# Planning a fused decoder block's TensorE order in whole groups, with a price for changing the kind of matmul and a new table of instruction lengths

## The chip, the core and the metric

The kernel runs on one core of a Trainium2 chip. The core has five instruction streams that run side by side and wait for each other through semaphores: TensorE (PE in the profile, with its weight loads as PEld), VectorE (DVE), ScalarE (ACT), GpSimd (POOL) and SyncE (SP). SP and POOL issue the DMAs. Each stream executes its instructions strictly in the order in which the program lists them, so an instruction that waits holds up everything behind it on its engine. The metric is the time of one execution on the device in microseconds (us), the median of several runs.

## The reference

One layer of a hybrid decoder: a pooling mixer and a gated DeltaNet side by side, on 2048 tokens of width 1024, all in float32.

```python
n    = rms_norm(x, norm_w)
proj = n @ w_in                      # 24 column tiles of 128, and 8 gate columns
pu, pz, q, k, v, dz, b, a = split(proj)

# pooling branch: 4 groups of 128 channels, trailing windows 2, 4, 8, 16
mix    = trailing_mean(pu, w) - pu
y_pool = (mix @ pool_w[g]) * pool_scale * silu(pz)

# DeltaNet branch: 4 heads of 128
q, k, v = split(silu(causal_conv4(q, k, v)))
q, k    = l2_normalize(q), l2_normalize(k)
beta, g = sigmoid(b), -exp(a_log) * softplus(a + dt_bias)
o       = gated_delta_rule(q, k, v, g, beta)   # chunked, a triangular solve per chunk
y_dn    = rms(o) * norm_w * silu(dz)

h   = x + concat(y_pool, y_dn) @ w_out
out = rms_norm(h, final_norm_w)
```

The chunked rule computes, per chunk and head, a triangular matrix A = strict_lower(k_beta k^T * decay), its inverse T = (I + A)^-1, and then steps a 128 x 128 state from chunk to chunk: v_new = u - w S, o = q_dec S + qk v_new, S = S * decay + k_dec^T v_new.

## The kernel before, in words

The tokens are worked in two blocks of 1024, each in two halves of 512. For each of the 24 column tiles of the input projection and each half, a unit of 8 steps (one for each 128 rows of the weight, `project`, L623) accumulates a 128 x 512 result in one PSUM bank. Each operand is split into a high and a low float32r part, so a step is three matmuls: high weight by high input (L629), high weight by low input (L630), low weight by high input (L631). These wide float32r matmuls are the bulk of TensorE's work. The output projection at the end is made of the same triples (L1164 to L1166 for the first four token tiles, L1278 to L1280 for the others, which are worked in pairs with seven products in place of eight).

Between the units lies the DeltaNet work of each head. Its matmuls are of two other kinds. Full-width float32 matmuls and transposes have 128 output partitions: the transposes of k, q, v and of the output (L719, L930), the products k k^T and k q^T (L745, L783), and the steps of the state from chunk to chunk, `chain_k`, `chain_u` and `chain_s` (L884 to L910). A float32 matmul stands in the trace as two records, a transpose as one. Narrow matmuls write to 32 or 64 partitions: they build the triangular inverse from its 32 x 32 blocks in five groups per head, `level1_y` (L839, 32 records), `level1_x` (L851, 32 records), `level2_t` (L863, 8), `level2_y` (L870, 16) and `level2_x` (L877, 16). The inverse of the 32 x 32 blocks themselves is done on VectorE (L799, L805), between two trips through DRAM (`scatter`, L762 and L765, and `gather`, L817 and L822) that rearrange the blocks.

The order of the work is not the order of the source. Every piece is put on a list with `at(slot, fn, ...)`; such an entry is an event. A slot is one step of a unit. `trace_events` (L599) runs the events in order of slot, which emits all instructions in program order. Then `Planner.run` (L151) makes an order for every engine by a simulation of its own: `costs` (L119) says for each instruction how long it holds its engine and after how long its result can be used, `preds` holds what must be finished first, `begun` what must have been started first. PSUM writes into the same bank depend on each other in it, so that the next matmul of a unit counts as ready some 440 ns after the one before. `propose` (L241) picks the next instruction of an engine. For TensorE it looks at the ready instructions in program order, no further than REACH = 200 TensorE instructions beyond the first one not yet placed, and takes the first that is ready within 30 ns, each matmul by itself (L254). For the other engines it goes by latest start times that are worked back from TensorE's program order. `bind` (L316) then fixes the orders found, for all five engines. The plan decides orders alone; on the chip the semaphores decide the times.

Some buffers tie the heads together: k, q, z and the inverse have two buffers each, the values and outputs of a head (`v0`) one, so the next head's values are written only when the head before has been stored.

Of the kernel before, what the change touches and what calls it, by code (L numbers as in the profile page):

```python
# [8 lines left out]
F32R = mybir.dt.float32r  # L9
# [5 lines left out]
P = 128  # L15
# [5 lines left out]
HALF = 512  # L21
# [60 lines left out]
HOP, REACH, SLACK, AHEAD = 40, 200, 100, 30000  # L82
# [3 lines left out]
class Planner:  # L86
# [4 lines left out]
    def __init__(self, tc, traced):  # L91
        self.tc = tc
        self.behind, self.next_to = {}, {}
        self.psum = set()
        self.rings = {}
        self.traced = traced

# [21 lines left out]
    def costs(self, i, outs, ins):  # L119

        op, eng = i.opcode, i.engine.name
        n = 1
        for _, c in outs[0].bass_ap.ap[1:]:
            n *= c
        psum = any(a.bass_ap.tensor.name in self.psum for a in (*outs, *ins))
        if op == "DMACopy":
            total = n * outs[0].bass_ap.ap[0][1] * 4 / 1024
            run = min(a.bass_ap.ap[-1][1] if a.bass_ap.ap[-1][0] == 1 else 1 for a in (outs[0], ins[0])) * 4
            land = 2200 + total * (5.5 if run >= 512 else 8)
            if eng == "Pool":  # L130
                return (860, 2900 + total * 5.4) if len(ins) > 1 or str(i.cce_op) != "bypass" else (600, 2400 + total * 3)
            return 550, land
        if eng == "PE":
            full = ins[0].dtype == F32R
            if full:
                return max(n / 2.4 + 13, 60), max(n / 2.4 + 190, 300)
            if getattr(i, "is_transpose", False):
                return (110, 290) if n > 64 else (56, 235)
            return (max(1.71 * n, 62), max(1.7 * n + 180, 240)) if n < 512 else (860, 1040)
        if eng == "Activation":  # L140
            extra = 190 if len(outs) > 1 else 0
            base = (150 if psum or extra else 110) + 0.82 * n
            return base + extra, base + extra + 110
        if eng == "Pool":
            return (650, 700) if op == "TensorScalarAffineSelect" else (2.5 * n + 100, 2.5 * n + 150)
        if op == "StreamTranspose":
            return 1.2 * n + 30, 1.2 * n + 130
        base = (68 if op == "TensorTensor" else 122 if n > 8 else 78) + 1.05 * n
        return base, base + 95

    def run(self):  # L151
        L = [i for i in self.traced if i.engine.name in self.ENGINES and (len(i.outs) or len(i.ins))]
        L = [i for i in L if i.opcode not in ("TilePoolBoundary", "TileManualSchedule")]
        N = len(L)
# [3 lines left out]
        for k, i in enumerate(L):  # L158
# [10 lines left out]
            if i.opcode == "DMACopy" and str(i.cce_op) != "bypass":  # L169
                acc.append((outs[0], False))  # L170
            for a, w in acc:
# [6 lines left out]
                if name in every:  # L178
                    begun[k].add(every[name][0])
                    if name in self.psum and w:  # L180
                        begun[k].add(next((j for j in reversed(every[name]) if eng[j] == eng[k]), every[name][0]))
# [52 lines left out]
        pe = [k for k in range(N) if eng[k] == "PE"]  # L234
        head = 0
        done = [False] * N
        lag = 0.0
        left = N
        proposal = {}

        def propose(e):  # L241
            c = cand[e]
            if not c:
                return None
            f = free[e]
            if e == "PE":
                lim = pe[min(head + REACH, len(pe) - 1)]
                c.sort()
                best = None
                for k in c:  # L250
                    if k > lim:
                        break
                    r = max(f, ready[k])
                    if r <= f + 30:  # L254
                        return r, k
                    if best is None or r < best[0]:
                        best = (r, k)
                return best
# [4 lines left out]
            u = min(c, key=lambda k: late[k])  # L263
# [15 lines left out]

        dirty = set(self.ENGINES)  # L280
        while left:
# [4 lines left out]
            at, k = proposal[e]  # L286
            cand[e].remove(k)
            order[e].append(k)
            start[k] = at
            done[k] = True  # L290
            left -= 1
            s = step[k]
            if e == "Activation" and table[k] and table[k] != act:
                act = table[k]
                s += 1283
                at += 1283
            free[e] = start[k] + s
            fin = at + lat[k] + HOP
            if e == "SP":
                lanes.append(fin)  # L300
            if e == "PE":
                lag = max(0.0, at - late[k]) if k == pe[head] else lag
                while head < len(pe) and done[pe[head]]:
                    head += 1
            dirty.add(e)
            for nexts, when in ((succs[k], fin), (after[k], at)):
                for j in nexts:
                    ready[j] = max(ready[j], when)
                    waiting[j] -= 1
                    if not waiting[j]:  # L310
                        cand[eng[j]].append(j)
                        dirty.add(eng[j])
# [12 lines left out]
def hymba_kernel(  # L325
# [273 lines left out]
    def trace_events():  # L599
        for _, _, fn, args in sorted(events, key=lambda e: e[:2]):  # L600
            fn(*args)
# [807 lines left out]
```

## Time and profile before

| | |
|---|---|
| median of 3 runs | 1005.52 us (997.4 to 1012.31) |
| the profiled execution: device time | 1004.09 us |
| its span, first to last instruction | 1002.4 us |
| outside the span (the difference) | 1.7 us |
| mean granted TensorE clock | 0.983 |
| TensorE busy | 950.6 us of the span |
| VectorE, ScalarE, GpSimd busy | 647.8, 474.5, 149.6 us |

In the views, a row of the timeline gives the start and the length in us, the engine, the line, the operation, output and inputs, their shapes and how many instructions were merged into the row. A matmul's length there includes its way through the array, so two that follow each other overlap: the time that one costs is the distance from its start to the next one's start. A row of the groups by line gives the busy time of the group, the mean length of one in ns, and the idle time of the engine before them.

### The profile page before, as it was taken

What the parts mean: (1) busy time and instruction counts of PE and PEld (TensorE: products, weight loads), DVE (VectorE), ACT (ScalarE), POOL (GpSimd) and SP (SyncE); (2) the same over time, 40 slices, a digit from 0 to 9 for tenths busy, and PEclk for the clock granted to TensorE, in tenths of its full rate; (3) what the DMA queues carried; (4) which work ended last, traced back from release to release, by engine and by line L of the source; (5) the groups of instructions that cost most, each with busy time, mean ns of one, the idle gap of its engine ahead of it and who ended that gap; (6) DMA issues with size and microseconds to landing.
All of it is one profiled execution on the core that took longest, in us unless ns stands there. A gap on an engine that the chain in (4) does not pass through costs nothing.

```text
span 1002.4 us, 14877 instructions
## 1 busy us (share of the span) xinstructions
PE 950.6 (95%) x5180; PEld 754.5 (75%) x5180; DVE 647.8 (65%) x1954; ACT 474.5 (47%) x1212; POOL 149.6 (15%) x200
## 2 busy tenths in 40 slices
PE   4999989999999899999999999899999998899995
PEld 3768767878888678767888878778868776688884
DVE  6477765758658436765885875756824467758765
ACT  7337653455464435433855445445423334344442
POOL 3204300100101012202520010110001110011111
PEclk9999989999999899999999999999999999999998
DMA  7322543423533634533445343253347486457644
GB/s 253 77 56 56 113 106 65 80 68 90 111 79 66 167 96 121 121 79 65 109 91 116 69 100 69 64 111 79 68 99 203 138 231 209 147 137 163 176 102 127
DMA packets 80396, 112.17 MB, mean 112 GB/s; under 512 B 31680, under 2 KB 49344, under 8 KB 80320
## 3 DMA queue, kind: packets, MB, share of 16 engines
q0 software_dynamic: 18000, 59.25, 28.5%
q1 hardware_dynamic: 62320, 51.96, 17.2%
q8 instruction: 41, 0.67, 0.3%
q14 instruction: 35, 0.29, 0.1%
HBM read 92.31 MB, written 18.87 MB: 111 GB/s over the span
## 4 chain that ended last, share of the span: by engine, by line
PE 68%; DVE 9%; DMA 9%; issue 8%; ACT 2%; SPq 1%; POOL 1%; DVEq 0%; POOLq 0%; ACTq 0%
PE ps L629 14%; PE ps L631 14%; PE ps L630 14%; DMA wh<-in_w_in_dram 2%; PE tp L719 2%; PE ch L906 1%; PE ch L900 1%; PE ch L884 1%; PE ob L894 1%; PE kk L745 1%; PE p L877 1%; DVE acc L643 1%; PE ob L910 1%; PE psA L1278 1%; PE pm L692 1%
## 5 line engine op out<-in xcount | busy, mean ns | idle before, releaser
L629 PE MATMUL ps<-nh,wh 128*128 128x512 f32 x768 | 293.6, 422 | 13.9 <-ACT wh L617 10.8
L631 PE MATMUL ps<-nh,wl 128*128 128x512 f32 x768 | 294.8, 421 | 1.9 <-DMA wl<-in_w_in_dram 1.3
L630 PE MATMUL ps<-nl,wh 128*128 128x512 f32 x768 | 290.8, 418 | 0.0
L629 PEld LDWEIGHTS ps<-nh,wh 128*128 128x128 f32 x768 | 144.6, 192 | 43.6 <-ACT wh L617 11.2
L631 PEld LDWEIGHTS ps<-nh,wl 128*128 128x128 f32 x768 | 146.8, 192 | 31.2 <-DMA wl<-in_w_in_dram 2.2
L630 PEld LDWEIGHTS ps<-nl,wh 128*128 128x128 f32 x768 | 145.9, 192 | 27.7 <-issue 1.7
L643 DVE SCALAR_TENSOR_TENSOR acc<-u,cw,acc 128x512 f32<-128x512 f32 x144 | 110.7, 769 | 14.8 <-ACT acc L641 13.2
L612 POOL DMA_DIRECT2D wh<-in_w_in_dram x46 | 26.2, 569 | 347.7 <-PE ps L630 240.6
L621 POOL DMA_DIRECT2D wl<-in_w_in_dram x46 | 39.3, 855 | 250.9 <-ACT wl L620 173.7
L799 DVE TENSOR_TENSOR tmp<-Ai,X 128x60 f32<-128x60 f32 (+24 forms) x248 | 53.6, 216 | 13.1 <-DMA Ai<-blocks 7.8
L620 ACT ACTIVATE wl<-wh 128x1024 fp32r<-128x1024 f32 x46 | 48.6, 1057 | 19.1 <-DMA wh<-in_w_in_dram 15.9
L805 DVE TENSOR_TENSOR X<-X,tmp 128x60 f32<-128x60 f32 (+24 forms) x248 | 53.0, 214 | 5.7
L638 DVE TENSOR_TENSOR u<-ps,rb 128x512 f32<-128x512 f32 x48 | 33.0, 688 | 35.6 <-PE ps L631 33.2
L913 ACT ACTIVATE sqj<-v 128x128 f32<-128x128 f32 x64 | 19.7, 307 | 67.5 <-DVE v L911 57.3
L641 ACT ACTIVATE acc<-u,cw 128x512 f32<-128x512 f32 x48 | 34.9, 726 | 25.6 <-DVE u L638 22.5
L726 ACT ACTIVATE sqj<-tp 128x128 f32<-128x128 f32 x128 | 33.8, 277 | 13.7 <-PE tp L719 13.0
L896 ACT ACTIVATE o<-ob,ex 128x128 f32<-128x128 f32 x64 | 23.4, 366 | 32.1 <-PE ob L894 31.5
L1173 ACT ACTIVATE t<-dec 128x512 f32<-128x512 f32 x32 | 20.2, 631 | 38.8 <-DVE dec L1171 38.5
L886 DVE SCALAR_TENSOR_TENSOR rho<-ch,negc,v 128x128 f32<-128x128 f32 x64 | 22.3, 348 | 24.4 <-PE ch L884 22.6
L1286 POOL DMA_DIRECT2D dec<-in_x_dram x24 | 20.5, 853 | 117.5 <-ACT dec L1285 98.6
L902 ACT ACTIVATE nv<-ch,sm 128x128 f32<-128x128 f32 x64 | 23.4, 366 | 26.0 <-PE ch L900 24.3
L748 DVE SCALAR_TENSOR_TENSOR At<-kk,sm,dec 128x128 f32<-128x128 f32 x64 | 18.2, 345 | 26.3 <-PE kk L745 26.2
(289 smaller groups left out, 1801.9 us busy)
## 6 DMA issues: line engine op xcount, KB each, us to landing
wh<-in_w_in_dram POOLq DMA_DIRECT2D x46, 512.0 KB, 3.9
wl<-in_w_in_dram POOLq DMA_DIRECT2D x46, 512.0 KB, 5.5
y_dram<-yt SPq DMA_DIRECT2D x32, 256.0 KB, 3.3
out_dram<-dec SPq DMA_DIRECT2D x14, 512.0 KB, 3.3
dec<-in_x_dram POOLq DMA_DIRECT2D x24, 256.0 KB, 4.0
Ai<-blocks SPq DMA_DIRECT2D x32, 128.0 KB, 2.7
dec<-in_xT_dram SPq DMA_DIRECT2D x7, 512.0 KB, 5.5
yr<-y_dram SPq DMA_DIRECT2D x6, 512.0 KB, 4.9
```

The costliest lines, as they stand in the source:

```text
L612: nc.gpsimd.dma_start(w["hi"], w_in[et])
L620: nc.scalar.activation(w["lo"], w["hi"].bitcast(F32), AF.Copy, scale=-1.0)
L621: nc.gpsimd.dma_start(w["lo"], w_in[et], accum_op=ALU.add)
L629: nc.tensor.matmul(ps, w["hi"][:, k], nh[:, k], start=(k == 0), stop=False)
L630: nc.tensor.matmul(ps, w["hi"][:, k], nl[:, k], start=False, stop=False)
L631: nc.tensor.matmul(ps, w["lo"][:, k], nh[:, k], start=False, stop=(k == KT - 1))
L638: nc.vector.tensor_tensor(out=ub[:, HALO:], in0=ps, in1=rb, op=ALU.mult)
L641: nc.scalar.activation(acc, ub[:, HALO:], AF.Copy, scale=cw[:, ci, CONV - 1 : CONV])
L643: nc.vector.scalar_tensor_tensor(out=acc, in0=ub[:, h0 + j : h0 + j + HALF], scalar=cw[:, ci, j : j + 1], in1=acc, op0=ALU.mult, op1=ALU.add,)
L726: nc.scalar.activation(junk, tp[:, j], AF.Square, accum_out=dst[:, c : c + 1])
L799: nc.vector.tensor_tensor(out=tmp[:, 0:n, 0:w], in0=Ai[:, j, j + 1 : BS].unsqueeze(1).to_broadcast([P, n, w]), in1=X[:, 0:n, j : j + 1].to ...
L805: nc.vector.tensor_tensor(out=X[:, 0:n, j + 1 : BS], in0=X[:, 0:n, j + 1 : BS], in1=tmp[:, 0:n, 0:w], op=ALU.subtract)
```

## The change

Five things change, all in the planner; no computation, buffer or slot does.

- TensorE is planned in groups: all the TensorE instructions of one event that follow each other make a run, and a run is placed as a whole, when everything it needs from outside is ready (each instruction's need is counted from its own place within the run, `lead`). `marks` records where events begin.
- Each run has a kind: "r" for float32r, "q" for an output with fewer than 128 partitions, "f" for the rest. `turn` gives the time that is added in the plan when a run follows one of another kind: 95 ns from r to q, 90 ns from q to r, 88 ns from f to r, nothing for other pairs. The first run in program order that can begin within TURN = 60 ns is taken; if there is none, the one that can begin earliest.
- REACH counts runs now: 24 beyond the first not yet placed.
- `costs` is a new table, for every engine and for the DMAs.
- A reader of a PSUM tile now also waits, in the plan, until the instruction of its own engine before it on that tile has begun (before, writers alone).

```diff
-HOP, REACH, SLACK, AHEAD = 40, 200, 100, 30000
+HOP, TURN, REACH, SLACK, AHEAD = 40, 60, 24, 100, 30000
...
         if op == "DMACopy":
-            total = n * outs[0].bass_ap.ap[0][1] * 4 / 1024
-            run = min(a.bass_ap.ap[-1][1] if a.bass_ap.ap[-1][0] == 1 else 1 for a in (outs[0], ins[0])) * 4
-            land = 2200 + total * (5.5 if run >= 512 else 8)
+            kb = n * outs[0].bass_ap.ap[0][1] / 256
             if eng == "Pool":
-                return (860, 2900 + total * 5.4) if len(ins) > 1 or str(i.cce_op) != "bypass" else (600, 2400 + total * 3)
-            return 550, land
+                return 600, (2900 + 5.3 * kb if self.adds(i) else 2300 + 3.1 * kb)
+            if type(outs[0].bass_ap.tensor).__name__ != "Tile" or outs[0].bass_ap.tensor.name.startswith(DRAM_TILES):
+                return 500, 1800 + 4.7 * kb
+            return 550, 2300 + 12.5 * min(kb, 256) + 1.7 * max(0, kb - 256)
         if eng == "PE":
-            full = ins[0].dtype == F32R
-            if full:
-                return max(n / 2.4 + 13, 60), max(n / 2.4 + 190, 300)
+            if ins[0].dtype == F32R:
+                return max(n / 2.4 + 13, 60), max(n / 2.4 + 193, 280)
             if getattr(i, "is_transpose", False):
-                return (110, 290) if n > 64 else (56, 235)
-            return (max(1.71 * n, 62), max(1.7 * n + 180, 240)) if n < 512 else (860, 1040)
+                return (110, 290) if n > 64 else (58, 235)
+            if n == 1:
+                return 223, 376
+            return (860, 1040) if n == HALF else (max(1.71 * n, 63), max(1.71 * n + 182, 237))
         if eng == "Activation":
-            extra = 190 if len(outs) > 1 else 0
-            base = (150 if psum or extra else 110) + 0.82 * n
-            return base + extra, base + extra + 110
+            scaled = len(outs) > 1 or len(ins) > 1
+            t = 170 + 0.6 * n if psum else 93 + 0.85 * n + 95 * scaled
+            return t, t + 108
         if eng == "Pool":
-            return (650, 700) if op == "TensorScalarAffineSelect" else (2.5 * n + 100, 2.5 * n + 150)
+            t = {"TensorScalarAffineSelect": 620}.get(op, 0.95 * n if op == "Memset" else 2.5 * n + 20)
+            return t, t + 30
         if op == "StreamTranspose":
-            return 1.2 * n + 30, 1.2 * n + 130
-        base = (68 if op == "TensorTensor" else 122 if n > 8 else 78) + 1.05 * n
-        return base, base + 95
+            return 464, 450
+        if op in ("TensorTensor", "TensorCopy"):
+            t = 70 + 1.04 * n
+        else:
+            t = 125 + 1.05 * n if n >= P else 78 + n
+        return t, t + 98
...
-                    if name in self.psum and w:
+                    if name in self.psum:
...
-        pe = [k for k in range(N) if eng[k] == "PE"]
...
+        runs, run_of = [], {}
+        for k in range(N):
+            if eng[k] == "PE":
+                if not runs or event[runs[-1][0]] != event[k]:
+                    runs.append([])
+                run_of[k] = len(runs) - 1
+                runs[-1].append(k)
+        kind = lambda k: "r" if L[k].ins[0].dtype == F32R else "q" if len(L[k].outs[0].bass_ap.ap) and L[k].outs[0].bass_ap.ap[0][1] < P else "f"
+        turn = {("r", "q"): 95, ("q", "r"): 90, ("f", "r"): 88}
+        kinds = [kind(r[0]) for r in runs]
...
+            if e == "PE":
+                best = None
+                for r in sorted(open_runs):
+                    if r > head + REACH:
+                        break
+                    when = max(f + turn.get((last, kinds[r]), 0), due[r])
+                    if when <= f + TURN:
+                        return when, r
+                    if best is None or when < best[0]:
+                        best = (when, r)
+                return best
...
-            if e == "PE":
-                lim = pe[min(head + REACH, len(pe) - 1)]
-                c.sort()
-                best = None
-                for k in c:
-                    if k > lim:
-                        break
-                    r = max(f, ready[k])
-                    if r <= f + 30:
-                        return r, k
-                    if best is None or r < best[0]:
-                        best = (r, k)
-                return best
...
+                    elif run_of.get(k) != r:
+                        due[r] = max(due[r], when - lead[j])
+                        short[r] -= 1
+                        if not short[r]:
+                            open_runs.append(r)
+                            dirty.add("PE")
...
+            if e == "PE":
+                r, last = k, kinds[k]
+                open_runs.remove(r)
+                gone[r] = True
...
+                for k in runs[r]:
+                    order[e].append(k)
+                    done(k, at)
+                    at += step[k]
+                    left -= 1
+                free[e] = at
+                continue
...
         for _, _, fn, args in sorted(events, key=lambda e: e[:2]):
+            plan.marks.append(len(plan.traced))
             fn(*args)
```

75 lines of the change are left out of this document (47 added, 28 removed).

## The prediction

> **What bounds the kernel now.** I read the page first: the busy times and the chain that ended last.
>
> ```profile
> span 1002.4 us, 14877 instructions
> PE 950.6 (95%) x5180; PEld 754.5 (75%) x5180; DVE 647.8 (65%) x1954; ACT 474.5 (47%) x1212; POOL 149.6 (15%) x200
> PE 68%; DVE 9%; DMA 9%; issue 8%; ACT 2%; SPq 1%; POOL 1%; DVEq 0%; POOLq 0%; ACTq 0%
> ```
>
> TensorE is busy for 950.6 of 1002.4 us and holds 68% of the chain. The kernel is bound by the length of TensorE's queue. A new order can save in three places: in the 51.8 us that TensorE idles, in what its queue loses between instructions, and in the stretches of halved clock. So I looked at the idle end (windows) and at what TensorE waited for (waits).
>
> ```profile
> 991.20:1002.40 11.20, 0.00 (x0) 0.00 (x0) 6.23 (x32) 2.89 (x7) 0.00 (x0) 0.71 0.26 95
> PE ps L629 <- ACT wh L617: 10.8, 2, 10.4
> PE y L839 <- DVE td L831: 2.9, 1, 2.9
> ```
>
> In a windows row the busy times stand in the order PE, PEld, DVE, ACT, POOL, then the granted clock and the DMA share. 10.4 us are the wait for the first weights (the longest wait of its row), 11.2 us the tail after the last matmul. The change touches neither, so 51.8 - 10.4 - 11.2 = 30.2 us of idle time are left in the middle, in many small waits.
>
> Then the timeline of TensorE, for what is lost inside the 950.6 us. First two wide matmuls to a row, then one narrow group (level2_x, L877) cut into four by wide matmuls, then the same group of another head left whole.
>
> ```profile
> 215.21 0.62 PE L629 MATMUL ps<-nh,wh 128*128 128x512 f32 x2
> 215.67 0.62 PE L630 MATMUL ps<-nl,wh 128*128 128x512 f32 x2
> ...
> 219.31 0.44 PE L877 MATMUL p<-Tt,t 64*64 64x64 f32 x4
> 219.68 0.50 PE L629 MATMUL ps<-nh,wh 128*128 128x512 f32 x1
> 220.11 0.44 PE L877 MATMUL p<-Tt,t 64*64 64x64 f32 x4
> 220.48 0.51 PE L630 MATMUL ps<-nl,wh 128*128 128x512 f32 x1
> 220.92 0.44 PE L877 MATMUL p<-Tt,t 64*64 64x64 f32 x4
> 221.29 0.50 PE L631 MATMUL ps<-nh,wl 128*128 128x512 f32 x1
> 221.72 0.44 PE L877 MATMUL p<-Tt,t 64*64 64x64 f32 x4
> 222.09 0.71 PE L745 MATMUL kk<-kT 128*128 128x128 f32 x4
> ...
> 284.75 1.14 PE L877 MATMUL p<-Tt,t 64*64 64x64 f32 x16
> 285.82 0.50 PE L630 MATMUL ps<-nl,wh 128*128 128x512 f32 x1
> ```
>
> A wide matmul among its like costs (215.67 - 215.21) / 2 = 0.23 us. Four narrow records hold the queue for 219.68 - 219.31 = 0.37 us, sixteen for 285.82 - 284.75 = 1.07 us: (1.07 - 0.37) / 12 = 0.058 us a record, and 0.37 - 4 x 0.058 = 0.14 us for entering and leaving. The wide matmul between two pieces takes 220.11 - 219.68 = 0.43 us, 0.20 more than its due. **A cut through a narrow group costs 0.14 + 0.20 = 0.34 us.** This is the loss that the change goes for.
>
> **The change part by part.**
>
> *Narrow groups whole.* There are 8 heads with five narrow groups, 40 events. I counted, in the timeline, the pieces in which they stand now: L839 in 12, L851 in 19, L863 in 11, L870 in 11, L877 in 24, 77 in all. The first and the last of them:
>
> ```profile
> 140.86 1.09 PE L839 MATMUL y<-td,At 32*32 32x32 f32 x32
> 752.47 0.44 PE L877 MATMUL p<-Tt,t 64*64 64x64 f32 x4
> ```
>
> As an event is now placed in one piece, 77 - 40 = 37 cuts go: 37 x 0.34 = **12.6 us**, all in TensorE's queue, which is the path. If the cuts through the 32-partition groups are cheaper (I priced one group of the 64-partition kind), it is some 2 us less.
>
> The plan's prices would let a narrow group save more where it stands beside a full-width float32 group, for which `turn` has no entry: 40 x 0.095 = 3.8 us. The trace has 222.09 - 221.72 = 0.37 us for the narrow piece ahead of L745, the same as ahead of a wide matmul, so I count nothing for it. [...]
>
> *Full-width float32 groups whole.* Transposes cut singly or in pairs by wide matmuls:
>
> ```profile
> 208.40 0.38 PE L719 MATMUL tp<-cst,vT 128*128 128x128 f32 x2
> 208.54 0.48 PE L631 MATMUL ps<-nh,wl 128*128 128x512 f32 x1
> 208.86 0.38 PE L719 MATMUL tp<-cst,vT 128*128 128x128 f32 x2
> ...
> 212.06 0.61 PE L719 MATMUL tp<-cst,kT 128*128 128x128 f32 x4
> 212.43 0.48 PE L630 MATMUL ps<-nl,wh 128*128 128x512 f32 x1
> ```
>
> Two transposes hold the queue for 208.54 - 208.40 = 0.14 us, four for 212.43 - 212.06 = 0.37, so two more cost 0.23. From pair to pair 208.86 - 208.40 = 0.46 us pass, and 0.23 of that is the wide matmul's due, 0.23 the transposes': within the rows' last digit, 0.01 us, a cut costs nothing. By the code there are 36 such events in each of 8 heads and 28 others (pooling, norms, gates), 316, against 462 pieces that I count in the timeline. 146 cuts x 0.01 = **1.5 us**, between 0 and 3. The plan's 88 ns for going back to float32r is many times what these rows show; it makes the plan bunch such groups, which costs nothing by itself since something ready is run in the meantime.
>
> *What whole groups cost.* A run waits for its last operand. Three cases. A triple waits for its low weight at its start, where before its two high products could go ahead: of these 46 + 4 tiles
>
> ```profile
> L621 POOL DMA_DIRECT2D wl<-in_w_in_dram x46 | 39.3, 855 | 250.9 <-ACT wl L620 173.7 <-ACT nv L902 27.1 <-ACT sqj L913 21.3
> L1101 POOL DMA_DIRECT2D wl<-y_dram x4 | 3.5, 873 | 26.8 <-ACT wl L1100 26.8
> ```
>
> I find the low part landing after the first high matmul in 6, and two matmuls went ahead then: 6 x 2 x 0.23 = 2.8 us at the most; I take 1, as another unit's triples stand within the 24 runs. A chain step (two matmuls) waits for both of its operands and for the end of a triple that is running: 0.2 us on average, on 192 steps, off the path as long as wide work fills TensorE meanwhile, and 192 x 0.2 / 8 = 5 us later for each head if it doesn't. A narrow run is put off while float32r runs are ready, up to the next full-width run or 24 runs (24 x 3 x 0.23 = 17 us); full-width runs are frequent where these groups stand (208.40 to 212.06 above). A head gets later by some microseconds, which its chain of steps, spread out by the slots, can make good.
>
> *The table.* Nearly all new numbers are nearer to the trace. The largest move on ScalarE is the sum of squares, 445 ns in the old table and 247 in the new one: one and the reading of its sum
>
> ```profile
> 161.25 0.27 ACT L726 ACTIVATE sqj<-tp 128x128 f32<-128x128 f32 x1
> 161.50 0.28 ACT L726 ACTIVATE sqj<-tp 128x128 f32<-128x128 f32 x1
> ...
> blocks<-At SPq DMA_DIRECT2D x32, 32.0 KB, 2.6
> inv<-X SPq DMA_DIRECT2D x32, 32.0 KB, 2.2
> ```
>
> comes back after 161.50 - 161.25 = 0.25 us. For the two DMAs, both before a narrow group, it goes the wrong way: 2.46 us before, 1.95 us now, 2.6 and 2.2 in the trace. That speaks for somewhat later narrow groups than planned. I set the table's effect on the 30.2 us of waits at nothing, between -15 (half of them gone, as the plan's clock is nearer to the chip's) and +12 (four more waits like the 2.9 us above).
>
> *Sum.* 1002.4 - 12.6 - 1.5 + 1 = 989.3 us of span; with the 1.7 us outside it, **991 us**. The profiled execution (1004.1) lies 1.4 us under the median of the three, so this is 992 in the median's terms, 1.3% less. I take the round 990.
>
> **The clock.** It is a separate term, since the order decides it. The trace has a granted clock of one half in some stretches. Windows of 3.41 us, set to its steps:
>
> ```profile
> 282.53:285.94 3.41, 3.41 (x38) 2.88 (x38) 1.95 (x11) 2.29 (x12) 0.00 (x0) 1.00 0.65 127
> 337.14:340.56 3.42, 1.32 (x19) 0.74 (x18) 0.06 (x1) 0.00 (x0) 0.00 (x0) 1.00 0.99 193
> 340.56:343.97 3.41, 2.64 (x22) 2.28 (x23) 1.84 (x4) 0.73 (x2) 0.00 (x0) 0.50 0.14 43
> 142.58:146.00 3.42, 2.96 (x45) 2.26 (x43) 2.40 (x6) 2.12 (x6) 0.56 (x1) 1.00 0.27 74
> 146.00:149.41 3.41, 3.41 (x21) 2.55 (x20) 2.82 (x7) 1.40 (x4) 0.00 (x0) 0.50 0.24 84
> ```
>
> After a window with little work the next one runs at half speed, and loses up to 1.7 us of work. It need not be an idle window: the one before 146.00 was busy for 2.96 us, but mostly with narrow matmuls. The one at 282.53, with a whole L877 in it, cost nothing after. The mean clock of 0.983 makes it 0.017 x 1002 / 0.5 = 34 us at half speed, a few of them in the tail, so up to some 14 us lost. [...]
>
> **The rivals.**
> 1. *Waits shrink too* (0.22). The plan's clock has the changes of kind in it, so groups reach the front of the queue when their operands do. For: a wait that becomes a half clock is paid twice (2.9 us at 341, then two such windows). Against: the slots and the uncovered DMA times stay. Half of the 30.2 us and a third of the clock's 14: 990 - 15 - 5 = 970 us.
> 2. *The clock takes the gain* (0.20). Whole narrow groups stand close together, with transposes between, and more windows look like that before 146.00. For: five windows are lost that way around narrow groups or their waits now, with about 4 windows per head, 32 in all, in danger. Against: 282.53. Eight more lost windows give 8 x 1.7 = 14 us back: 1004 us, no change.
> 3. *Slower* (0.11). A narrow group, whole, comes to the front of TensorE's queue before its operand, everything wide stands behind it, and the window so emptied halves the clock: at 341, the case that the waits show, 2.9 us of wait and 2 x 1.7 of clock, 6.3 us. Before, half the group had at least gone ahead. For: the shortened DMA times ahead of L839. Against: one case in eight heads now. The third such head takes the gain, the sixth makes it slower by 2%: with six, 990 + 38 = 1028 us.
> 4. *The change does little of what it says* (0.02): the order is bound on the engine, so an event cannot be cut.
>
> **How the numbers follow.** The forecast has 0.45: cuts gone, waits and clock as now within 8 us, 982 to 998. The range takes in the bounds of the waits, the first rival down to 968, the second, and the lower part of the third up to 1016; about 0.1 lies beyond each end. A difference under 2%, 20 us, can't be told from none here, as the runs of before spread over 15 us: faster means under 985.4. That holds for all of the first rival and a third of the forecast's range: 0.37. Slower means over 1025.6: most of the third rival, and some of what I have not thought of: 0.11. No change: 0.52.
>
> **What would show it.** The five narrow lines stand in 40 pieces or fewer (right), with 1.07 us from the start of an L877 group to the next wide matmul; full-width ones in 316 pieces or fewer. TensorE's busy time falls by 12 to 14 us if the first step is right, whatever the waits do. Idle time in the middle well over 30 us, with L839 or L851 as waiters, shows the third rival; a mean clock under 0.975 the second. I am wrong if the pieces are 40 and the busy time has not fallen: then a cut costs less than its rows say, or the time came back as half clock.

## The result and the profile after

The changed kernel takes 976.19 us (median of 4 runs, 973.08 to 978.8) beside 1003.78 us for the kernel before (4 runs, 997.4 to 1012.31): a ratio of 0.9719, 95% interval 0.9639 to 0.9798. It is faster by 27.6 us, twice the 14 us that I forecast. All ratios and intervals here leave out the few runs that fell in a slower state; the medians of the experiments include them. The profiled execution took 973.08 us; before, 1004.09. Added code moves the line numbers by 50 or 51: L629 to L631 are now L680 to L682, L839 is L890, L851 is L902, L877 is L928, L884 to L910 are L935 to L961, L1164 to L1166 are L1215 to L1217.

The page of the kernel after: the span, the busy times, the granted clock in 40 slices, and the chain that ended last.

```profile
span 971.4 us, 14859 instructions
PE 924.1 (95%) x5180; PEld 742.5 (76%) x5180; DVE 651.8 (67%) x1954; ACT 470.1 (48%) x1210; POOL 151.9 (16%) x200
PEclk9999999999999999999999999999999999999998
PE 71%; DVE 10%; issue 9%; DMA 5%; ACT 3%; POOL 1%; SPq 1%; DVEq 0%; POOLq 0%; ACTq 0%
```

The bound is the same, TensorE's queue, at 95% busy. But its busy time fell by 26.5 us, from 950.6 to 924.1. The idle time in the middle fell too: with 12.1 us of wait for the first weights and 11.1 us of tail, 971.4 - 924.1 - 12.1 - 11.1 = 24.1 us are left, where there were 30.2. The row of the clock, in tenths over 40 slices, is all nines up to the tail. The same row of the page before has two eights more, in the slices that hold the half-speed windows at 146.00 and 340.56 of the prediction:

```profile
PEclk9999989999999899999999999999999999999998
```

In all, TensorE ran at half clock for 27.3 us between start and tail before, in six stretches, and for 6.8 us after, in one. A look at the narrow groups in the timeline of the kernel after, first two groups of 32 partitions, then one of 64:

```profile
139.87 1.09 PE L890 MATMUL y<-td,At 32*32 32x32 f32 x32
140.89 0.50 PE L680 MATMUL ps<-nh,wh 128*128 128x512 f32 x1
...
143.15 1.09 PE L902 MATMUL xx<-Tt,td 32*32 32x32 f32 x32
144.18 0.50 PE L680 MATMUL ps<-nh,wh 128*128 128x512 f32 x1
...
216.08 1.14 PE L928 MATMUL p<-Tt,t 64*64 64x64 f32 x16
217.15 1.60 PE L796 MATMUL kk<-kT 128*128 128x128 f32 x12
```

Every narrow group stands whole, 40 pieces in all, eight for each of the five lines, and L928 holds the queue for 217.15 - 216.08 = 1.07 us. Full-width float32 groups stand in 235 pieces (462 before). From here on, pieces are counted in the program's order, and two different groups that stand side by side count as one: by that count the kernel before has 75 narrow pieces, where the prediction, line by line, has 77; the cuts through groups are 37 in either case.

To see where the 31.0 us of the two spans went, I added up, over all 5180 TensorE records, the distance from each start to the next one's, and took off what that kind of matmul costs among its like (0.227 us for a wide one, 0.11 for a full-width float32 record, 0.03 to 0.06 for a narrow one). What is left is loss, sorted by where it lies. The same account is given here for the experiments that are told below.

```
loss, us              before  after | narrow  narrow  wide    before    after
                                    | whole   cut     single  one line  one line
narrow groups, edges    20.8   10.5 |  11.6    26.5    11.1     10.2      10.7
full-width groups       10.2   12.2 |  10.4    10.6    10.1      9.3      13.8
wide among wide         10.5    7.8 |   9.4    10.0    10.3      7.3       7.0
at half clock           13.9    1.7 |   6.7    35.3    11.2     16.5       6.2
starts that waited      38.3   28.8 |  34.2    38.9    42.3     27.2      19.1
```

(A start that waited is one after more than 60 ns of idle; its row has the whole loss of that start in it, so it is larger than the idle time, 38.3 us beside 30.2 before and 28.8 beside 24.1 after. What is lost in a stretch at half clock stands in that row alone, cuts included. The account is of the profiled run of each kernel, one run each.) From before to after: 10.3 us less at the narrow groups, 12.2 us less at half clock, 9.4 us less in waits, 2.8 us less among the wide matmuls and 2.0 us more at the full-width groups, 32.7 in all, against 1.7 us more of wait for the first weights.

### The profile page after: what moved, and what is told of

The parts are those of the page before. It is cut to its first block, busy times and chain, and to the rows that moved or that the text cites. A ratio compares the mean times of both kernels' runs of the same rounds, so it can differ in the third digit from the quotient of the medians.

```text
span 971.4 us, 14859 instructions
## 1 busy us (share of the span) xinstructions
PE 924.1 (95%) x5180; PEld 742.5 (76%) x5180; DVE 651.8 (67%) x1954; ACT 470.1 (48%) x1210; POOL 151.9 (16%) x200
## 4 chain that ended last, share of the span: by engine, by line
PE 71%; DVE 10%; issue 9%; DMA 5%; ACT 3%; POOL 1%; SPq 1%; DVEq 0%; POOLq 0%; ACTq 0%
PE ps L680 14%; PE ps L682 14%; PE ps L681 14%; PE tp L770 2%; PE ch L957 2%; DVE X L856 2%; DVE tmp L850 2%; PE ch L935 1%; DVE acc L694 1%; PE psA L1329 1%; PE psA L1330 1%; PE psA L1331 1%; PE ob L945 1%; PE ch L951 1%; PE ob L961 1%
## 5 line engine op out<-in xcount | busy, mean ns | idle before, releaser
L680 PE MATMUL ps<-nh,wh 128*128 128x512 f32 x768 | 325.7, 424 | 12.4 <-ACT wh L668 12.1
L681 PE MATMUL ps<-nl,wh 128*128 128x512 f32 x768 | 300.9, 392 | 1.5 <-DVE nl L494 1.5
L682 PE MATMUL ps<-nh,wl 128*128 128x512 f32 x768 | 301.7, 393 | 0.0
L680 PEld LDWEIGHTS ps<-nh,wh 128*128 128x128 f32 x768 | 145.4, 189 | 37.4 <-ACT wh L668 12.1
L682 PEld LDWEIGHTS ps<-nh,wl 128*128 128x128 f32 x768 | 144.5, 188 | 32.0 <-DVE wl L478 0.3
L953 ACT ACTIVATE nv<-ch,sm 128x128 f32<-128x128 f32 x64 | 23.6, 369 | 28.8 <-PE ch L951 28.5
L958 DVE SCALAR_TENSOR_TENSOR state<-state,ex,ch 128x128 f32<-128x128 f32 x64 | 22.0, 344 | 21.0 <-PE ch L957 19.8
L705 DVE TENSOR_TENSOR szp<-ps,rb 128x512 f32<-128x512 f32 x16 | 11.0, 687 | 33.0 <-PE ps L682 33.0
L1217 PE MATMUL pso<-nh,wl 128*128 128x512 f32 x64 | 25.9, 405 | 7.3 <-DMA wl<-y_dram 7.3
L957 PEld LDWEIGHTS ch<-nv,kdec 128*128 128x128 f32 x128 | 19.7, 188 | 16.8 <-ACT nv L953 16.2
```

Source lines behind the costliest of these rows:

```text
L680: nc.tensor.matmul(ps, w["hi"][:, k], nh[:, k], start=(k == 0), stop=False)
L681: nc.tensor.matmul(ps, w["hi"][:, k], nl[:, k], start=False, stop=False)
L682: nc.tensor.matmul(ps, w["lo"][:, k], nh[:, k], start=False, stop=(k == KT - 1))
L957: nc.tensor.matmul(ch[:, 2], e["kdec"][:, c], nv, start=True, stop=True)
```

## The experiments

**Narrow groups alone, whole and then cut.** The first kernel has the changed planner's machinery with every rule of the kernel before (its table, REACH 200, 30 ns of tolerance, no prices); only the narrow events are kept as runs, every other matmul is a run by itself. The second cuts these runs after four matmuls and lets the plan avoid following one piece by another, so that wide matmuls come between.

```diff
+    narrow = L[k].ins[0].dtype != F32R and L[k].outs[0].bass_ap.ap[0][1] < P
-    if not runs or event[runs[-1][0]] != event[k]:
+    if not runs or event[runs[-1][0]] != event[k] or not narrow:
         runs.append([])
... the second, on top of the first
-    if not runs or event[runs[-1][0]] != event[k] or not narrow:
+    if not runs or event[runs[-1][0]] != event[k] or not narrow or len(runs[-1]) == 4:
-turn = {}
+turn = {("q", "q"): 300}
```

> The kernel of before with one thing changed: the matmuls of a narrow group stay together (75 pieces become 40); everything else is planned one matmul at a time with the old table and no prices. By the prediction's first term, 35 or 37 cuts at 0.34 us: 12 us less than before, 991 us, with waits and clock as before. If the narrow groups are also what costs the half clock, the clock rises to 0.99 as well and the time is 980 us.

> The kernel of before with the narrow groups cut on purpose after every four matmuls, so that they stand in 112 pieces (75 before, 40 in e4_narrow_alone); table, prices and all else as before. If a cut costs 0.25 to 0.34 us in TensorE's queue and nothing else (the prediction's first term), 72 cuts more than e4 are 18 to 24 us: 1003 to 1009 us. If cut groups are also what halves the clock (theory two, by the runs so far: 0.989 with 40 pieces, 0.983 with 75, 0.970 with 91), the mean clock falls to 0.965 or less, which is 15 us more: 1018 to 1030 us.

Lines move here too: L676 to L678 are the triple, L886 is `level1_y`, L898 `level1_x`. Whole: 984.78 us, ratio 0.9841 [0.9742, 0.9939], with 40 narrow pieces and 469 full-width ones. Cut: 1029.99 us, ratio 1.0211 [1.0119, 1.0302], with 112 narrow pieces. The pages have

```profile
span 980.8 us, 14873 instructions
PE 931.9 (95%) x5180; PEld 747.1 (76%) x5180; DVE 648.9 (66%) x1954; ACT 474.5 (48%) x1212; POOL 149.5 (15%) x200
```

for the whole groups and, for the cut ones,

```profile
span 1030.2 us, 14877 instructions
PE 977.9 (95%) x5180; PEld 770.0 (75%) x5180; DVE 648.4 (63%) x1954; ACT 476.3 (46%) x1212; POOL 150.0 (15%) x200
```

So whole narrow groups alone give, by the medians, somewhat more than half of the gain (the interval leaves anything from a fifth to nearly all), and 72 cuts more cost 3.7%. Of the 49.4 us between these two spans 46.0 lie in TensorE's busy time. Its timeline in the kernel with cut groups shows what a cut costs, and its windows show what else it costs:

```profile
142.41 0.43 PE L886 MATMUL y<-td,At 32*32 32x32 f32 x8
142.77 0.49 PE L678 MATMUL ps<-nh,wl 128*128 128x512 f32 x1
143.20 0.43 PE L886 MATMUL y<-td,At 32*32 32x32 f32 x8
143.56 0.50 PE L676 MATMUL ps<-nh,wh 128*128 128x512 f32 x1
```

```profile
142.59:146.01 3.42, 3.40 (x44) 2.17 (x41) 1.65 (x5) 2.17 (x4) 0.55 (x1) 1.00 0.49 151
146.01:149.42 3.41, 3.41 (x19) 1.85 (x17) 3.41 (x6) 0.75 (x2) 0.00 (x0) 0.50 0.03 7
```

From piece to piece 143.20 - 142.41 = 0.79 us pass, of which 0.23 are the wide matmul's and 8 x 0.032 = 0.26 the narrow records' (in the rows of after, (140.89 - 139.87) / 32 = 0.032): a cut through a 32-partition group costs 0.30 us in the queue, nearly the 0.34 of the 64-partition group in the prediction. By that, 72 cuts are 22 to 24 us. The other part is the clock. The window from 142.59 is busy for 3.40 of 3.42 us, but only four of its 44 matmuls are wide, and the window behind it runs at half speed. In the account the cut groups lose 14.9 us more at their edges at full clock, and 28.6 us more at half clock, a part of the cuts among them. The mean clock of the timed runs, beside that of the kernel before (75 pieces) on the same chip, was 0.968 against 0.976 with 112 pieces; with 40 it was 0.9855 against 0.984, which the scatter of the runs covers. **The 72 cuts were paid twice, once in the queue and once in the clock**; that the step from 75 pieces to 40 moves the clock is not shown by these timed runs.

**The table.** One kernel is the kernel before with the new table (and with the new rule for readers of PSUM); the other is the changed kernel with the old table.

```diff
 the kernel before
-    def costs(self, i, outs, ins):      # old
+    def costs(self, i, outs, ins):      # new
-                    if name in self.psum and w:
+                    if name in self.psum:
... the changed kernel
-    def costs(self, i, outs, ins):      # new
+    def costs(self, i, outs, ins):      # old
```

> The plan of before, one matmul at a time and without prices, with the new table of lengths and the new rule for readers of PSUM, but neither groups nor prices. If the gain of 28 us is the whole groups' (theory one), the narrow groups stand in about 80 to 90 pieces as before and the time is within 8 us of before, about 1004 us. If the new lengths make the waits and the half clock smaller (theory two), the idle time in the middle falls by 6 us or more, the mean clock rises to about 0.99, and the time is 985 to 990 us.

> The changed kernel with the table of lengths of before: groups and prices alone. Theory one: 40 narrow pieces, all of the gain on them stays; about 978 us if the table does nothing. Theory two: the cuts are gone (10 us) but waits and half clock come back (16 us): about 990 us, mean clock 0.983 to 0.985.

The table alone makes the kernel slower, which neither of my two sums had: 1018.34 us, 1.0167 [1.008, 1.0253]; the profiled run's row of the cores is

```profile
core 0: 1020.6 us, clock 0.970
```

with 91 narrow pieces in place of 75. Sixteen more cuts, at the 37 us for 72 that the two kernels above are apart, make some 8 of the 17 us; where the rest comes from is open. The profiled run stood at half clock for 54.6 us between start and tail, the kernel before for 27.3. The groups without it are as good as with it, within the intervals: 977.5 us, 0.9778 [0.9716, 0.9841]. What the whole change gains does not come from the table.

**The prices, and the full-width groups.** The changed kernel without the prices, and that kernel with the full-width float32 matmuls placed one by one.

```diff
-turn = {("r", "q"): 95, ("q", "r"): 90, ("f", "r"): 88}
+turn = {}
... the second, on top of the first
+    full = L[k].ins[0].dtype != F32R and L[k].outs[0].bass_ap.ap[0][1] == P
-    if not runs or event[runs[-1][0]] != event[k]:
+    if not runs or event[runs[-1][0]] != event[k] or full:
```

> The changed kernel with no price for a change of kind (groups and new table stay). Theory one: 40 narrow pieces, so within 4 us of the changed kernel, about 976 to 980 us; the pieces of full-width matmuls rise from 235 to some 280 and cost nothing. If the prices are what brings the operands in time, waits come back: 985 us or more.

> e3_no_prices with the full-width float32 matmuls planned one by one again (pieces from 281 to 332); triples and narrow groups stay whole. By the prediction's second term a cut there costs nothing to 0.02 us: within 5 us of e3, 974 to 979 us. If these cuts are what the rest of the gain (974 against the 985 of e4_narrow_alone) comes from: about 980 us.

973.94 us, 0.9742 [0.9672, 0.9813], with 281 full-width pieces, and 975.63 us, 0.9695 [0.9624, 0.9766], with 332. Neither can be told from the changed kernel (235 pieces), though with 51 cuts more a price of 0.1 us for each would still hide in the intervals. The account bounds it closer: the full-width groups lose 10.2 us in 462 pieces and 12.2 us in 235, so no price of a cut shows there.

**A wait ahead of the narrow groups.** The third rival needs a narrow group that waits at the front of the queue. Eight VectorE instructions that multiply `td`, the operand of L890, by one stand between its transposes and `level1_y` in each head, and the plan counts them as nothing. I had set them at some 3 us a head; by the pages VectorE is busy for 669.9 us in place of 651.8, which is 0.28 us for each and 2.3 us a head. They leave the result as it is.

```diff
     (level1_t, behind the transposes)
+    for i in range(8):
+        o = 2 * BS * (i % 2)
+        nc.vector.tensor_scalar(out=td[o : o + BS], in0=td[o : o + BS], scalar1=1.0, scalar2=None, op0=ALU.mult)
     (costs)
+    if eng == "DVE" and outs[0].bass_ap.tensor.name.startswith("td") and op != "StreamTranspose":
+        return 0, -HOP
```

> The changed kernel with eight VectorE instructions, some 3 us together, between the transposes (L831 of before) and level1_y in each of the 8 heads; the plan is not told of them, so TensorE's order stays and each whole narrow group comes to the front of the queue about 3 us before its operand. The prediction's third rival prices such a wait at 2.9 us and two windows at half clock, 6.3 us: 8 x 6.3 = 50 us more, 1026 us, mean clock 0.965. If a wait costs only itself, 8 x 2.5 to 3 = 20 to 24 us, 998 us, mean clock 0.99.

981.39 us, 0.9759 [0.9699, 0.982]: by the medians 5 us more than the changed kernel, which the intervals don't tell from none, and not the 50 that 8 waits of 3 us with two half-clock windows each would cost. The waits of TensorE in that kernel (engine, tile, line, releaser: sum, times, longest; its L1222 and L962 are L1217 and L957 of the changed kernel):

```profile
PE pso L1222 <- DMA wl<-y_dram: 7.4, 2, 6.3
PE ch L962 <- ACT nv L958: 3.1, 1, 3.1
...
PE xx L907 <- ACT td L899: 1.6, 1, 1.6
```

`level1_y` is not among them, since in the changed kernel the transposes are done 2.5 to 8.5 us before it starts, in all eight heads. The plan's order had cover there, so the experiment did not make the waits that it was meant to make, and neither of its two sums was tested as written. The one new wait is at `level1_x` (L907), 1.6 us up to 519.4, in the window

```profile
516.42:519.84 3.42, 1.78 (x21) 1.20 (x21) 3.39 (x9) 2.04 (x8) 0.84 (x1) 1.00 0.42 55
```

and the three windows behind it, 519.8 to 530.1, ran at half clock: with up to 1.7 us lost in each, that is an estimated 6.7 us with the wait, beside the third rival's price of 6.3. It came once.

**Wide matmuls one by one.** The changed kernel without prices, with every float32r matmul a run by itself and REACH at 72 (three times as many runs).

```diff
-    if not runs or event[runs[-1][0]] != event[k]:
+    if not runs or event[runs[-1][0]] != event[k] or L[k].ins[0].dtype == F32R:
-... REACH ... = ... 24 ...
+... REACH ... = ... 72 ...
```

> e3_no_prices with the wide float32r matmuls planned one by one again, within a reach of 72 of them (the same stretch as 24 triples); full-width and narrow groups stay whole, and so do the new lengths. If whole triples bring the rest of the gain over e4_narrow_alone: 983 to 987 us. If they bring nothing: 974 to 978 us.

995.72 us (10 runs), 0.9914 [0.9874, 0.9953], beyond both of my sums: most of the gain is gone, although the narrow groups are whole. So the whole triples, which I had down as a cost of 1 us, are worth 17 us by the ratios and 22 by the medians beside the new table. Under the old table they are worth less: from narrow groups alone (0.9841) to all groups (0.9778) it is some 6 us, within the intervals, triples, prices and full-width groups together. The waits grew,

```profile
PE ch L957 <- ACT nv L953: 8.2, 7, 2.2
PE pso L1217 <- DMA wl<-y_dram: 8.2, 1, 8.2
PE ps L682 <- DMA wl<-in_w_in_dram: 3.2, 2, 2.0
PE y L890 <- DVE td L882: 2.5, 1, 2.5
```

where the changed kernel has

```profile
PE pso L1217 <- DMA wl<-y_dram: 7.3, 2, 6.0
PE ch L957 <- ACT nv L953: 3.1, 1, 3.1
```

and 11.2 us are lost at half clock (1.7 in the changed kernel), with 40 narrow pieces in either: cuts are not all that moves the clock.

**What makes the plan cut and wait: a wait inside the plan.** The three matmuls of a triple write the same PSUM bank, and in the plan each counts as ready only about 440 ns after the one before has begun (403 + 40 in the old table). On the chip no such time passes. In the changed kernel a triple follows itself at the pace of any wide matmuls:

```profile
139.09 0.39 PE L680 MATMUL ps<-nh,wh 128*128 128x512 f32 x1
139.32 0.39 PE L681 MATMUL ps<-nl,wh 128*128 128x512 f32 x1
139.55 0.39 PE L682 MATMUL ps<-nh,wl 128*128 128x512 f32 x1
```

With that wait the plan sees a hole of 0.2 us after each wide matmul (443 ns less the 226 that it holds the engine), and fills it: with a wide matmul of another unit, or with a piece of a narrow group. A run hides the wait inside itself, and keeps it between runs. The last four kernels take it out: a TensorE instruction that uses what another TensorE instruction wrote needs that one begun, not finished, which the order of the queue gives: the three starts above are 0.23 us apart.

```diff
-                        p.add(j)
+                        (begun[k] if eng[j] == eng[k] == "PE" else p).add(j)
```

This line goes into the changed kernel without prices, into the kernel with wide matmuls one by one, into the kernel before, with nothing else, and into the changed kernel.

> e3_no_prices with one condition changed in the plan: a TensorE matmul no longer counts as waiting 440 ns for the TensorE matmul before it on the same PSUM bank, only for its start (the engine works in order anyhow). So the triples of a unit follow each other, and units come one after another. If what the whole triples bring is fewer units open at once (1.74 of them on average before, 1.75 in e4, 1.80 in e8, 1.5 in the changed kernel and in e3), the waits shrink again: 962 to 970 us. If the two units side by side are of use (a slower evacuation is spread better): 978 us or more.

> e8_wide_single (wide matmuls planned one by one, 996 us) with the same condition changed. If e8 lost its 22 us against e3 by the units open at once, they come back: 965 to 978 us, waits down from 35 to 25 us or less. If it lost them because a triple is torn apart: 990 us or more.

> The kernel of before with this one condition changed: no groups, no prices, the old table. The narrow pieces fall from 75 to 41 of themselves, the full-width ones from 462 to 281. If the false wait in the plan is the common cause of the cuts and of the units open at once, this alone gives what the whole change gives: 968 to 980 us. If whole groups, prices or table are needed beside it: 985 us or more.

> The changed kernel, prices and all, with the one condition of e10_no_self_wait: TensorE does not wait for itself on a PSUM bank. If units one after another are what the rest of the gain comes from, the time is that of e10, 966 to 971 us, and the prices (the only difference from e10) are worth nothing, within 3 us. If the prices work against units that follow each other, 974 us or more.

```
                                    median us    ratio [95%]              narrow  units   us from first
                                    (lowest to highest)                   pieces  open    to last matmul
before                              1003.78                                 75    1.74        14.0
changed kernel                       976.19      0.9719 [0.9639, 0.9798]    40    1.51        11.4
  without prices                     973.94      0.9742 [0.9672, 0.9813]    40    1.49
  wide one by one                    995.72      0.9914 [0.9874, 0.9953]    40    1.80        14.5
the line on: without prices          968.97      0.9670 [0.9632, 0.9709]    40    1.01         7.3
             wide one by one         972.92      0.9705 [0.9657, 0.9753]    40    1.01
             before                  974.49      0.9739 [0.9694, 0.9784]    41    1.01         7.4
             changed kernel          964.24      0.9614 [0.9570, 0.9658]    40    1.01         7.0
```

(Units open: how many units of wide matmuls had begun and not ended at once, on the average, read from the program's order beside the trace. Each ratio is to runs of the kernel before on the same chip.)

With the line, the kernel before gains 2.6%, as much as the whole change. It cuts its narrow groups no more, 41 pieces, though nothing tells it not to. And with the line, wide matmuls one by one are nearly as good as in triples: 22.8 us of difference by the medians, 21 by the ratios, between the two kernels with the line and without it. Both have 40 narrow pieces, so here it is not the cuts that the line takes away. The waits of the one with the line, beside those of its like further up:

```profile
PE pso L1217 <- DMA wl<-y_dram: 6.0, 2, 3.7
PE ps L682 <- DMA wl<-in_w_in_dram: 2.9, 2, 1.7
PE ch L957 <- ACT nv L953: 1.3, 1, 1.3
```

The best version, the changed kernel with the line, came out below its 966 to 971 us: it is 4.7 us under the same kernel without prices. The two intervals overlap, so whether the prices are worth something beside the line stays open. The page of the kernel before with the one line (its profiled run was the slowest of its four, 979.64 us, and stood at half clock for 34.1 us, so its account has 16.5 us there in spite of 41 pieces),

```profile
span 977.9 us, 14855 instructions
PE 934.2 (96%) x5180; PEld 752.8 (77%) x5180; DVE 654.6 (67%) x1954; ACT 477.2 (49%) x1212; POOL 150.5 (15%) x200
```

and of the best version, 964.24 us (6 runs, 962.38 to 967.19, the slowest of them profiled; the changed kernel's own runs begin at 973.08):

```profile
span 965.5 us, 14862 instructions
PE 928.9 (96%) x5180; PEld 746.3 (77%) x5180; DVE 653.7 (68%) x1954; ACT 476.4 (49%) x1212; POOL 151.6 (16%) x200
```

Its gain over the changed kernel lies in the waits, 19.1 us in the account where there were 28.8; in the profiled run 4.5 us more at half clock take part of it back. One unit is now open at a time in place of one and a half, and a unit takes 7.0 us in place of 11.4. That banks and weight buffers come free earlier by this, and that the waits shrink for that reason, is what I take from it; no run tests that link by itself.

## Why the prediction was right and where not

The forecast was 990 us in a range of 968 to 1016, and 976 came out, within the range, 14 us under the forecast and nearer to the first rival's 970. The forecast's own band, 982 to 998, missed it, and the likeliest outcome by my chances, no change (0.52, against 0.37 for faster), did not come. The mechanism of the first term was right; the rest of the gain I had in a rival at 0.22, for another reason, so that the range held it is in part luck.

- **Narrow groups whole (12.6 us): right.** 40 pieces, 1.07 us from L928 to what follows, and a price of a cut of 0.30 to 0.34 us from the new rows. The account has 10.3 us at full clock. Where cuts stood in stretches at half clock before, their loss is in that row.
- **Full-width groups whole (1.5 us): no gain that shows.** 235 pieces, under the 316 that I gave as a bound; the account has 10.2 us at these groups before and 12.2 after. The lower end, 0, fits.
- **From one kind of matmul to another.** Going into a narrow group and coming back cost 0.30 to 0.34 us by the rows. Between full-width float32 and float32r, both 128*128 in the rows, the number of pieces (462 before, 235 after) does not show in the account, 10.2 and 12.2 us.
- **Whole triples (a cost of 1 us): wrong in sign.** I looked at what a triple must wait for and not at what its order sets free. Taken apart, beside the new table, the kernel is 17 to 22 us slower. The triples are what hides the plan's wait within a bank, and that wait I had before me in the code as "some 440 ns" without asking what the plan does with it. It is the step of the sum that failed.
- **The table (nothing, -15 to +12): right for this change**, where old and new table give the same; alone it is at +17 us, beyond the bound, in part by more cuts.
- **The clock as now: wrong, and the largest miss in the account.** The account has 13.9 us lost at half clock before, which was my bound of 14, and 1.7 after. I had priced a cut by the queue alone; 72 more cuts lost 28.6 us more at half clock than whole groups do. The profiled runs show more of it than the medians: over 33 runs of the kernel before, time and mean clock go together (994.29 us at 0.992, 1012.42 at 0.973, 7.6 us for 0.01, correlation -0.87), and from their mean clock of 0.979 to the changed kernel's 0.990 makes, by that slope, an estimated 8.4 of the 27.6 us. Which part of the change moved the clock is open: whole narrow groups alone did not move it beyond the scatter, and with whole narrow groups but single wide matmuls 11.2 us were still lost there.
- **The first rival** had the right pieces, waits and clock falling together, with 20 us for both; the account has 9.4 and 12.2. Its reason, that the plan's clock has the changes of kind in it, fell: without prices, or with the old table, the gain is the same within the intervals.
- **The second rival had the sign the wrong way round.** I feared that whole narrow groups, standing close, would empty more windows. A whole group of 1.07 us leaves unbroken wide work around it in the 3.41 us window; a cut group, with one wide matmul of 0.23 us in each 0.8, is the thin mix. The window at 282.53, which I had quoted against the rival, was the case to believe. That is shown where cuts are added (112 pieces), not for the 37 that the change takes away.
- **The third rival** had no place for its wait, and its price was met but once, by the 1.6 us of L907 and the three windows behind it: the changed plan keeps 2.5 us or more between the transposes and `level1_y`. I had not asked how much cover there is.
- **Busy time down by 12 to 14 us** "whatever the waits do": it fell by 26.5, since beside the cuts the half clock went, at which a wide matmul takes 0.43 us from start to start (150.25 to 150.68 in the kernel before) in place of 0.23. That test could not tell the cuts from the clock.

## What to carry to other kernels

Here the plan had some 440 ns between two TensorE matmuls on one bank, where the trace has 0.23 us from start to start: what they owed each other was their order and not a latency. A latency put there is filled with something, and what it is filled with (cuts through groups, a second unit opened) is what one then pays for. Price such a cut by the rows of the queue (0.30 to 0.34 us here) and then ask what the same stretch does to the clock (with 72 cuts more, 28.6 us more were lost at half clock). And try a plan's rule alone before believing that its numbers matter: here neither the new table nor the prices gave anything that shows in the change, and one line in the dependencies gave as much as the whole change.

## What the runs showed of the hardware

**In these traces half clock came behind windows with little full-width work, and not all of these were idle.** I cut the profiled runs of twelve kernels and of the kernel before, all of this study but the last, into windows of 3.413 us set to the steps of the clock (four of the six stretches at half clock in the kernel before are that long, the other two twice that), and added up for each the work of its full-width matmuls (0.227 us for a wide one, 0.11 for a float32 record or a transpose, narrow ones not counted). Of 3385 windows at full clock with at least 40% of such work, none was followed by half clock. Of 168 with less, 53 were: 23 of 41 with under 20%, 16 of 23 with 20 to 30%, 14 of 104 with 30 to 40%. At half clock, 39 of 50 windows with under 40% were followed by another, of 30 with 50% or more none (a wholly busy window at half clock comes to some 53% by this count). The bounds are those of these thirteen traces, and what made the other 115 windows harmless is open. The window at 142.59 further up was busy for 3.40 of its 3.42 us, and half clock came behind it. The one stretch that the changed kernel has left is an idle one, the 6.0 us wait of L1217 in its windows:

```profile
794.11:797.52 3.41, 0.91 (x4) 0.40 (x3) 3.41 (x4) 1.93 (x3) 0.00 (x0) 1.00 0.83 250
797.52:800.93 3.41, 0.00 (x0) 0.00 (x0) 1.08 (x3) 0.00 (x0) 0.00 (x0) 0.50 1.06 276
```

Its other long wait, the 3.1 us of L957 up to 737.96, did not move the clock. It begins in one window and ends in the next,

```profile
732.67:736.08 3.41, 2.20 (x11) 1.50 (x9) 1.45 (x3) 0.29 (x1) 0.00 (x0) 1.00 1.07 373
736.08:739.49 3.41, 1.53 (x10) 1.41 (x11) 1.01 (x3) 1.72 (x4) 0.86 (x1) 1.00 0.83 301
```

and either has some work left. In the kernel with the added VectorE instructions the same wait (L962 there, 3.1 us up to 744.89) lies within one window, and the next one runs at half clock:

```profile
741.69:745.10 3.41, 0.27 (x2) 0.21 (x2) 0.80 (x2) 1.31 (x2) 0.22 (x1) 1.00 1.06 368
745.10:748.51 3.41, 3.41 (x13) 3.02 (x13) 2.06 (x5) 0.77 (x3) 0.63 (x1) 0.50 0.91 217
```

So the same wait was paid once where it lay across two windows, and twice where it lay in one; these are two cases.

**The spread of the kernel before went with its clock.** The same program took 994.29 us at a mean clock of 0.992 and 1012.42 at 0.973, and over its 33 runs the correlation of the two is -0.87. The kernels that lost less at half clock were steadier, as far as so few runs tell: the changed kernel's four runs lie within 5.7 us, the best version's six within 4.8, three of the kernel with cut groups within 12.1.
